# Values of mixer D: blocks of consecutive tokens and a store and load through DRAM in place of strided columns

## The chip, the cores and the metric

The kernel runs on one core of a Trainium2 chip. The metric is the device time of one execution in microseconds (us). A core has a matrix engine (TensorE, PE in the profile, its loads of the stationary operand shown apart as PEld), a vector engine (DVE), a scalar engine (ACT), a general engine (POOL) and a queue engine (SP) that issues DMA transfers. Each engine works through its own instructions in order and waits on semaphores for the others.

## The reference

Two layers over 512 tokens of width 1024. A layer computes one wide projection, four mixers A, B, C and D, a gated sum of their projections, and an MLP. Only mixer D and its values matter here:

```python
proj = hn @ w_in[l]                      # dv: 3 groups x 4 heads x 64 = 768 columns of it
def mixer_d(q, k, v, cs):                # v: [b, s, 3 groups, 4 heads, 64]
    for gi, (window, dil) in enumerate(((128, 1), (512, 4), (2048, 16))):
        # tokens of one residue modulo dil attend to each other, in a band
        o, lse = banded_attention(to_residue(q), to_residue(k), to_residue(v), window // (2 * dil), 64)
    # groups combined by their softmax denominators
```

The first group uses the tokens in their natural order, the other two by residues.

## The kernel before

All products are done in parts: each operand is split into a high and a low part, and one product becomes three (high by high, high by low, low by high; lines 177 to 179 in `mm3`). The 1024 channels are 8 blocks of 128, so a full product is 24 matrix instructions. `xh` and `xl` hold the normed input, split, as [128 channels, 8 blocks, 512 tokens].

The weights come as a stream of chunks of 128 x 1024 (512 KB): a load on SP's queue into one of three raw buffers (`wload`, line 102), a cast by ACT that makes the high part (`whi`, line 118), and a subtraction by DVE that makes the low part (`wlo`, line 127). `take` hands a chunk out and issues the casts and loads that come next. There are three buffers of split chunks, so the cast of a later chunk waits until the chunk three places ahead of it is used up.

The layer has phases. In phase 1 the projections are made. Then each attention (A, C, D) is interleaved by `merge` with a "fill" of matrix products that do not depend on it: gates and branch projections of a mixer that is done. The interleave is counted: `MG` gives for each phase the attention's steps, the fill's steps and how many fill steps come ahead. In the phase of mixer C the fill is `values_d` followed by `fill(l, 0, yA)`, and the entry is (41, 73, 2).

`values_d` (line 669) makes the values of mixer D, three groups (two chunks of weights each, `take2`). In it the tokens are the stationary operand (the columns of `xh` that are loaded into the array) and the 256 value columns of the group are the moving one. A token chunk is one product of 24 instructions, in two fill steps of 12. The keys of each group lie in an own order of tokens, and the value rows are made directly in that order:

- first group: five chunks, of 64, 128, 128, 128 and 64 consecutive tokens (`off`, line 671);
- second and third group: four chunks each, every fourth token from residue c on (`slice(c, None, 4)`, line 679).

ACT takes each result out of PSUM into the tile `VD` with a factor per token (lines 685 and 686). PSUM gives these products two buffers in turn (`ps("mm")`). The factors lie in `roff` in the same orders as the tokens; `roff` is filled in phase 1 by three small loads from DRAM (lines 465 to 467). Attention D (`attn_d`) reads `VD` as stationary operand in the phase after that of mixer C (lines 992 and 998).

`fill` takes its gate tiles `gt` from a pool of five buffers (line 731). Loads of mixer C's queries (line 773) go through SP's queue between the weight loads.

Of the kernel before, what the change touches and what calls it, by code (L numbers as in the profile page):

```python
# [11 lines left out]
F32 = mybir.dt.float32  # L12
# [16 lines left out]
V_GMIX, V_GMLP, V_GB, V_CW, V_CB, V_LGB, V_LAM, V_G, V_SINK = 0, 8, 16, 48, 64, 68, 84, 92, 96  # L29
NV = 104  # L30
# [4 lines left out]
# attention of A and C: the stages of a step and how many steps each lags behind the first  # L35
# [4 lines left out]
# steps of an attention phase, steps of its fill, steps of the fill ahead of the first one  # L40
MG = ((35, 48, 3), (41, 73, 2), (18, 47, 12))
# waits in the end of mixer D, in steps of the fill beside it, and the steps of that fill
E1, E2, E3, FN = (1, 5, 2, 15)
# products that warm the tensor engine up; parts in which the first two chunks come
WU, P0, P1 = (16, 2, 2)
# the order of the projections; pieces of mixer B after each; projections that its gates follow
# [29 lines left out]
class Body:  # L76
# [29 lines left out]
    def parts(self, i):  # L106
        """the first chunk is worked on in parts, for an early start"""
        n = (P0, P1, 1)[min(i, 2)]
        return [slice(p * (1024 // n), (p + 1) * (1024 // n)) for p in range(n)]
# [20 lines left out]
    def ahead(self, i):  # L130
        """the high parts of the next groups, and the loads beyond them"""
        i -= self.held
        n = len(self.order)
        while self.n_split < min(i + self.HLB, n):
            self.whi()
        while self.n_load < min(self.n_lo + self.RAWB, n):
            self.wload()
# [5 lines left out]
    def take2(self, *key):  # L143
        """two chunks that stay for several groups"""
        return [self.take(*key, u, wide=u) for u in range(2)]
# [38 lines left out]
    def several(self, keys, mv, cuts):  # L184
        """the groups of some chunks, side by side: each part of the depth for all of them"""
        sts = [self.wst(self.take(*key, wide=u)) for u, key in enumerate(keys)]
        pss = [self.wide() for _ in keys]
        mm = self.nc.tensor.matmul
        for k0, k1 in zip((0,) + cuts, cuts + (KD,)):
            for st, ps in zip(sts, pss):  # L190
                for k in range(k0, k1):
                    (sh, sl), (mh, ml) = st(k), mv(k)
                    mm(ps, sh, mh, start=(k == 0), stop=False)
                    mm(ps, sh, ml, start=False, stop=False)
                    mm(ps, sl, mh, start=False, stop=(k == KD - 1))
        self.ahead(self.n_take)
        self.lows()
        return pss
# [22 lines left out]
    def rsqrt(self, v, n, tag):  # L221
        """v: [128, n] in SBUF, positive"""
        nv = self.nc.vector
        y, t = self.smt(n, tag + "y"), self.smt(n, tag + "t")
        yi = y.bitcast(I32)
        nv.tensor_scalar(out=yi, in0=v.bitcast(I32), scalar1=1, scalar2=None, op0=ALU.logical_shift_right)
        nv.tensor_scalar(out=yi, in0=yi, scalar1=-1.0, scalar2=float(0x5F3759DF), op0=ALU.mult, op1=ALU.add)
        for _ in range(3):
            nv.scalar_tensor_tensor(out=t, in0=y, scalar=-0.5, in1=y, op0=ALU.mult, op1=ALU.mult)
            nv.tensor_tensor(out=t, in0=t, in1=v, op=ALU.mult)  # L230
            nv.scalar_tensor_tensor(out=y, in0=t, scalar=1.5, in1=y, op0=ALU.add, op1=ALU.mult)
        return y

    def xg_tile(self, xt, c, gcol):
        """xt [128, 512] f32: tile c of the residual; writes xg"""
        nc = self.nc
        nc.scalar.activation(out=self.xh[:, c], in_=xt, func=AF.Copy, scale=gcol)
        nc.vector.scalar_tensor_tensor(
            out=self.xl[:, c], in0=xt, scalar=gcol, in1=self.xh[:, c].bitcast(F32), op0=ALU.mult, op1=ALU.subtract
        )  # L240
# [10 lines left out]
    def norm_cols(self):  # L251
        """1/rms of each token, as columns [128, 4]"""
        nc = self.nc
        ps = self.misc()
        for c in range(4):
            nc.tensor.matmul(ps[:, c:c + 1], self.acc[:, c * 128:(c + 1) * 128], self.ones[:, 0:1])
        v = self.smt(4, "nv")
        nc.vector.tensor_scalar(out=v, in0=ps[:, 0:4], scalar1=1.0 / DM, scalar2=EPS, op0=ALU.mult, op1=ALU.add)
        return self.rsqrt(v, 4, "n")
# [38 lines left out]
    def derive(self):  # L298
# [7 lines left out]
        # softplus(-lam) = max(-lam, 0) + log1p(exp(-|lam|)), log1p(u) = 2 atanh(u / (u + 2))  # L306
# [23 lines left out]
    # ================= projections of the mixers, and mixer B =================  # L330
    def rope(self, X1, X2, T, dst, split, perm=False):
        """X1, X2 in PSUM; T: the factors (of x1, of x2 in the first half; of x2, of x1 in the second)"""
# [64 lines left out]
    def phase1(self, l):  # L397
# [13 lines left out]
        self.kD = self.drp.tile([3, 4, 64, S], F32, tag="kD", name="kD")  # L411
        ckp, skp = self.table(4, "b0"), self.table(5, "b1")
# [12 lines left out]
        def head_scale(key, nh, sel, n=128):  # L425
            """1/rms of each head and token, but for the token's own factor: [128, 4 * nh]"""
# [21 lines left out]
        # the tokens' 1/rms, as columns, as a row, and over all partitions  # L448
# [12 lines left out]
        # tokens in other orders: by 64 from 64 on for the first group of D, by residues for the others  # L461
        rd = self.drp.tile([S], F32, tag="rd", name="rd")
        self.roff = self.mixp.tile([128, 16], F32, tag="roff", name="roff")
        nc.sync.dma_start(out=rd.rearrange("(o n) -> o n", o=1), in_=row)
        nc.sync.dma_start(out=self.roff[:, 8:12], in_=rd.rearrange("(p r) -> p r", r=4))
        nc.sync.dma_start(out=self.roff[:, 1:4], in_=rd[64:448].rearrange("(c p) -> p c", p=128))
        nc.sync.dma_start(out=self.roff[0:64, 0:5:4], in_=rd.rearrange("(c p) -> p c", p=64)[:, 0:8:7])
# [41 lines left out]
        # queries of C, queries and keys of D; gates of mixer B between them  # L509
# [16 lines left out]
        nv.tensor_scalar(out=self.rs8p, in0=self.roff[:, 8:12], scalar1=0.125, scalar2=None, op0=ALU.mult)  # L526

    def values_ac(self):
        """values of A and C: token-major, [hi | lo]"""
# [68 lines left out]
    def gates_b(self, f):  # L598
        """gates of a tile of mixer B; what follows goes to the queue"""
# [33 lines left out]
        def s2(f, d):  # L633
            q, a, u = bs[f, d]
            # 1 - a^2 = tanh(-log a) (1 + a^2)
            nv.scalar_tensor_tensor(out=q, in0=Tg[f, d, 0], scalar=1.0, in1=q, op0=ALU.add, op1=ALU.mult)
            nv.scalar_tensor_tensor(out=u, in0=u, scalar=1.0, in1=self.xcs[f], op0=ALU.add, op1=ALU.mult)
# [31 lines left out]
    def values_d(self):  # L669
        ns = self.nc.scalar  # L670
        off = ((0, 64), (64, 192), (192, 320), (320, 448), (448, 512))
        last = []
        for g in range(3):
            hls = self.take2("VD", g)
            for c in range(5 if g == 0 else 4):
                if g == 0:
                    sl, n, col = slice(*off[c]), off[c][1] - off[c][0], c
                else:
                    sl, n, col = slice(c, None, 4), 128, 8 + c
                ps = self.ps("mm")  # L680
                yield from self.paced(last, self.mm3(
                    ps[0:n, 0:256],
                    lambda k: (self.xh[:, k, sl], self.xl[:, k, sl]),
                    lambda k: tuple(t[:, (k % 4) * 256:(k % 4 + 1) * 256] for t in hls[k // 4]), KD, 4))
                last.append(lambda ps=ps, n=n, i=(0, 5, 9)[g] + c, col=col: ns.activation(
                    out=self.VD[0:n, i], in_=ps[0:n, 0:256], func=AF.Copy, scale=self.roff[0:n, col:col + 1]))
                yield
        while last:
            last.pop()()

# [8 lines left out]
    # ================= gates and projections of the branches =================  # L699
# [44 lines left out]
    # ================= attention =================  # L744
    def pipeline(self, steps, order):
        """steps: dicts of stages; order: (stage, its distance in steps from the first)"""
# [7 lines left out]
    def attn_gqa(self, l, which, y):  # L754
        """8 heads, 2 key heads. A: all keys; C: a band, with sinks"""
# [274 lines left out]
    def attn_d_end(self, y):  # L1030
        """the groups' weights: exp(m_g - M) / sum_g l_g exp(m_g - M)"""
# [57 lines left out]
    def merge(self, a, b, na, nb, first=0):  # L1089
        """a's first step, a few of b, then na steps of a spread over nb of b; then the rest"""  # L1090
# [19 lines left out]
    # ================= the layer =================  # L1110
    def layer(self, l):
# [99 lines left out]
        def last(h):  # L1211
            """the last two tiles and the final norm, by halves of the tokens"""
# [255 lines left out]
```

## Time and profile before

| | us |
|---|---|
| time, median of 3 runs | 2096.09 |
| lowest, highest | 2095.13, 2098.7 |
| span of the profiled execution, first to last instruction | 2091.4 |
| median less that span | 4.7 |
| PE busy | 2071.0 (99%) |
| PEld busy | 1711.7 (82%) |
| DVE busy | 1273.3 (61%) |
| ACT busy | 977.9 (47%) |
| DMA queue q1, share of 16 engines | 31.6% |

The profile is of one execution, and its span is what the rows below add up to; the time of a run also holds some us around it. Matrix instructions overlap: one is shown as 0.28 us long and the next starts 0.12 us after it. So the pace of TensorE is read from the starts of instructions that follow each other, not from their lengths. A wait in the profile names the waiting instruction, then what released it, the sum in us, how often, and the longest.

### The profile page before, as it was taken

Reading aid. Unit: us, or ns where it says so; the run is one execution under the profiler, and the core shown is the slowest. Engines: PE = TensorE matmul, PEld = TensorE weight load, DVE = VectorE, ACT = ScalarE, POOL = GpSimd, SP = SyncE. Lnnn points to the kernel's source line nnn. Section 1 sums busy time; section 2 is a strip of 40 time slices with the busy share of each in tenths; the row PEclk is TensorE's granted clock in tenths of the full one; section 3 lists DMA queues with packets and bytes.
Section 4 is the critical chain, followed back from the end, with each engine's and each line's share of the span. In section 5 each row is a group of like instructions: output and inputs, shape, how many; then the busy total and the mean of one; then the engine's idle time right before and its main releaser. Section 6 shows DMA issues by size and latency. Waiting matters only on the chain.

```text
span 2091.4 us, 25718 instructions
## 1 busy us (share of the span) xinstructions
PE 2071.0 (99%) x9800; PEld 1711.7 (82%) x9800; DVE 1273.3 (61%) x2274; ACT 977.9 (47%) x1703; POOL 0.2 (0%) x4
## 2 busy tenths in 40 slices
PE   9999999999999999999999999999999999999997
PEld 7888889987778888888878888898877788888886
DVE  6889774575466544444658887736644665444445
ACT  4366885663534332322323667757545343322322
POOL 0000000000000000000000000000000000000000
PEclk9999999999999999999999999999999999999999
DMA  5445313122234222222325552312321432223221
GB/s 190 156 142 159 113 54 100 59 97 95 72 100 144 95 97 94 97 93 99 133 95 171 159 163 67 101 66 66 121 81 53 135 117 93 99 93 99 93 100 61
DMA packets 83407, 220.74 MB, mean 106 GB/s; under 512 B 15674, under 2 KB 17850, under 8 KB 83284
## 3 DMA queue, kind: packets, MB, share of 16 engines
q1 hardware_dynamic: 80404, 214.91, 31.6%
q10 hardware_dynamic: 2880, 4.20, 0.6%
q8 instruction: 77, 1.26, 0.3%
q14 instruction: 46, 0.38, 0.1%
HBM read 197.94 MB, written 21.12 MB: 105 GB/s over the span
## 4 chain that ended last, share of the span: by engine, by line
PE 96%; DVE 2%; ACT 1%; issue 1%; DMA 0%; SPq 0%; DVEq 0%; ACTq 0%
PE ps_mm L177 15%; PE ps_mm L179 14%; PE ps_mm L178 14%; PE ps_t L177 6%; PE ps_t L179 6%; PE ps_t L178 6%; PE ps_s L177 6%; PE ps_s L179 6%; PE ps_s L178 6%; PE ps_o L846 2%; PE ps_t L825 2%; PE ps_s L786 1%; PE ps_s L787 1%; PE ps_o L992 1%; PE ps_t L966 1%; PE ps_s L917 1%
## 5 line engine op out<-in xcount | busy, mean ns | idle before, releaser
L118 ACT CAST whi<-raw 128x1024 fp32r<-128x1024 f32 (+1 forms) x318 | 329.9, 1042 | 353.6 <-PE ps_mm L178 122.0
L127 DVE TENSOR_TENSOR wlo<-raw,whi 128x1024 fp32r<-128x1024 f32 (+1 forms) x318 | 385.0, 1214 | 106.0 <-ACT whi L118 103.3
L177 PE MATMUL ps_mm<-xh,whi 128*128 128x512 f32 x720 | 288.2, 400 | 0.0
L179 PE MATMUL ps_mm<-xh,wlo 128*128 128x512 f32 x720 | 282.0, 392 | 0.0
L178 PE MATMUL ps_mm<-xl,whi 128*128 128x512 f32 x720 | 281.8, 391 | 0.0
L177 PEld LDWEIGHTS ps_mm<-xh,whi 128*128 128x128 f32 x720 | 135.5, 188 | 32.4 <-issue 4.1
L179 PEld LDWEIGHTS ps_mm<-xh,wlo 128*128 128x128 f32 x720 | 135.6, 188 | 29.3
L178 PEld LDWEIGHTS ps_mm<-xl,whi 128*128 128x128 f32 x720 | 135.8, 189 | 26.9
L177 PE MATMUL ps_t<-xh,whi 128*128 128x512 f32 x368 | 143.7, 390 | 0.0
L178 PE MATMUL ps_t<-xl,whi 128*128 128x512 f32 x368 | 143.2, 389 | 0.0
L179 PE MATMUL ps_t<-xh,wlo 128*128 128x512 f32 x368 | 143.2, 389 | 0.0
L177 PE MATMUL ps_s<-xh,whi 128*128 128x512 f32 x352 | 138.6, 394 | 0.0
L179 PE MATMUL ps_s<-xh,wlo 128*128 128x512 f32 x352 | 137.1, 389 | 0.0
L178 PE MATMUL ps_s<-xl,whi 128*128 128x512 f32 x352 | 137.0, 389 | 0.0
L835 DVE TENSOR_TENSOR PT<-ps_t,PT 128x512 fp32r<-128x512 f32 (+2 forms) x128 | 75.2, 588 | 72.2 <-ACT PT L832 56.6
L832 ACT CAST PT<-ps_t 128x512 fp32r<-128x512 f32 (+2 forms) x128 | 63.8, 501 | 57.5 <-PE ps_o L846 56.1
L819 ACT ACTIVATE P<-P,al 128x512 f32<-128x512 f32 (+2 forms) x128 | 82.7, 646 | 12.6 <-DVE al L818 11.6
L709 DVE TENSOR_TENSOR gt<-ps_mm,rb 128x512 f32<-128x512 f32 x54 | 37.2, 688 | 80.7 <-PE ps_mm L179 80.5
L177 PEld LDWEIGHTS ps_t<-xh,whi 128*128 128x128 f32 x368 | 69.1, 188 | 17.4 <-issue 3.0
L179 PEld LDWEIGHTS ps_t<-xh,wlo 128*128 128x128 f32 x368 | 69.1, 188 | 14.4
L178 PEld LDWEIGHTS ps_t<-xl,whi 128*128 128x128 f32 x368 | 69.1, 188 | 14.3
L177 PE MATMUL ps_mm<-whi,xh 128*128 128x256 f32 (+1 forms) x224 | 79.6, 355 | 0.0
(423 smaller groups left out, 4330.7 us busy)
## 6 DMA issues: line engine op xcount, KB each, us to landing
raw<-in_w_dram SPq DMA_DIRECT2D x314, 512.0 KB, 3.5
qsA<-stk SPq DMA_DIRECT2D x32, 128.0 KB, 2.3
qsC<-stk SPq DMA_DIRECT2D x32, 128.0 KB, 2.3
K<-ks SPq DMA_DIRECT2D x16, 256.0 KB, 5.6
Q<-qsA SPq DMA_DIRECT2D x16, 256.0 KB, 4.0
Q<-qsC SPq DMA_DIRECT2D x16, 256.0 KB, 2.7
qD<-stkf SPq DMA_DIRECT2D x24, 128.0 KB, 2.2
kD<-stkf SPq DMA_DIRECT2D x24, 128.0 KB, 2.2
```

Of the source, the lines that this page charges most:

```text
L118: self.nc.scalar.copy(hi[:, s], self.raws[i][:, s])
L127: self.nc.vector.tensor_tensor(out=lo[:, s], in0=raw[:, s], in1=hi[:, s].bitcast(F32), op=ALU.subtract)
L177: mm(ps, sh, mh, start=(k == 0), stop=False)
L178: mm(ps, sh, ml, start=False, stop=False)
L179: mm(ps, sl, mh, start=False, stop=(k == n - 1))
L709: nv.tensor_tensor(out=g, in0=ps, in1=self.rb, op=ALU.mult)
L786: nc.tensor.matmul(ps[:, 0:n], qq, Kt[j][:, 0, b0 * 128:b1 * 128], start=True, stop=False)
L819: ns.activation(out=P[:, 0:n], in_=P[:, 0:n], func=AF.Copy, scale=ls)
L825: nc.tensor.transpose(pt[:, b * 128:(b + 1) * 128], P[:, b * 128:(b + 1) * 128], self.ident)
L832: ns.copy(st["dst"][0], st["src"])
L835: nv.tensor_tensor(out=st["dst"][1], in0=st["src"], in1=st["dst"][0].bitcast(F32), op=ALU.subtract)
L846: nc.tensor.matmul(o, a, b, start=(n_ == 0), stop=(n_ == len(mm) - 1))
```

## The change

Every token chunk of `values_d` is now one of four blocks of 128 consecutive tokens, for all three groups. The result leaves PSUM by ACT into a staging tile `vst` (one of the five `gt` buffers, 256 of its columns) with the factor of the natural token order, `rcol`. SP stores it to a DRAM tensor `vD`. After the fourth chunk of a group SP loads the group back into `VD` in the order of its keys: two loads for the first group, one for each other group. `roff` shrinks to the four columns that attention D needs, and two of its three loads go. The fill's step count in `MG` goes from 73 to 71.

```diff
-MG = ((35, 48, 3), (41, 73, 2), (18, 47, 12))
+MG = ((35, 48, 3), (41, 71, 2), (18, 47, 12))
...
+        self.vD = self.drp.tile([3, S, 256], F32, tag="vD", name="vD")
...
-        self.roff = self.mixp.tile([128, 16], F32, tag="roff", name="roff")
+        self.roff = self.mixp.tile([128, 4], F32, tag="roff", name="roff")
         nc.sync.dma_start(out=rd.rearrange("(o n) -> o n", o=1), in_=row)
-        nc.sync.dma_start(out=self.roff[:, 8:12], in_=rd.rearrange("(p r) -> p r", r=4))
-        nc.sync.dma_start(out=self.roff[:, 1:4], in_=rd[64:448].rearrange("(c p) -> p c", p=128))
-        nc.sync.dma_start(out=self.roff[0:64, 0:5:4], in_=rd.rearrange("(c p) -> p c", p=64)[:, 0:8:7])
+        nc.sync.dma_start(out=self.roff, in_=rd.rearrange("(p r) -> p r", r=4))
...
-        nv.tensor_scalar(out=self.rs8p, in0=self.roff[:, 8:12], scalar1=0.125, scalar2=None, op0=ALU.mult)
+        nv.tensor_scalar(out=self.rs8p, in0=self.roff, scalar1=0.125, scalar2=None, op0=ALU.mult)
...
     def values_d(self):
-        ns = self.nc.scalar
-        off = ((0, 64), (64, 192), (192, 320), (320, 448), (448, 512))
+        nc = self.nc
         last = []
         for g in range(3):
             hls = self.take2("VD", g)
-            for c in range(5 if g == 0 else 4):
-                if g == 0:
-                    sl, n, col = slice(*off[c]), off[c][1] - off[c][0], c
-                else:
-                    sl, n, col = slice(c, None, 4), 128, 8 + c
+            for c in range(4):
                 ps = self.ps("mm")
                 yield from self.paced(last, self.mm3(
-                    ps[0:n, 0:256],
-                    lambda k: (self.xh[:, k, sl], self.xl[:, k, sl]),
+                    ps[:, 0:256],
+                    lambda k: (self.xh[:, k, c * 128:(c + 1) * 128], self.xl[:, k, c * 128:(c + 1) * 128]),
                     lambda k: tuple(t[:, (k % 4) * 256:(k % 4 + 1) * 256] for t in hls[k // 4]), KD, 4))
-                last.append(lambda ps=ps, n=n, i=(0, 5, 9)[g] + c, col=col: ns.activation(
-                    out=self.VD[0:n, i], in_=ps[0:n, 0:256], func=AF.Copy, scale=self.roff[0:n, col:col + 1]))
+                last.append(lambda ps=ps, g=g, c=c: self.value_d(ps, g, c))
                 yield
...
+    def value_d(self, ps, g, c):
+        nc = self.nc
+        t = self.gtp.tile([128, S], F32, tag="gt", name="vst", bufs=5)
+        nc.scalar.activation(out=t[:, 0:256], in_=ps[:, 0:256], func=AF.Copy, scale=self.rcol[:, c:c + 1])
+        nc.sync.dma_start(out=self.vD[g][c * 128:(c + 1) * 128], in_=t[:, 0:256])
+        if c < 3:
+            return
+        if g == 0:
+            nc.sync.dma_start(out=self.VD[:, 1:4], in_=self.vD[g][64:448].rearrange("(c p) n -> p c n", p=128))
+            nc.sync.dma_start(
+                out=self.VD[0:64, 0:5:4], in_=self.vD[g].rearrange("(c p) n -> p c n", p=64)[:, 0:8:7]
+            )
+        else:
+            o = (5, 9)[g - 1]
+            nc.sync.dma_start(out=self.VD[:, o:o + 4], in_=self.vD[g].rearrange("(p r) n -> p r n", r=4))
```

The rest of the diff takes comments and docstrings out.

## Rows read from the trace of the kernel before

**Rows 1.** Page, part 4: the chain that ended last, share by engine.
```profile
PE 96%; DVE 2%; ACT 1%; issue 1%; DMA 0%; SPq 0%; DVEq 0%; ACTq 0%
```

**Rows 2.** Waits of PE, whole span: us in total, times, longest.
```profile
PE ps_s L786 <- DMA Q<-qsA: 5.6, 2, 3.4
...
PE ps_s L1256 <- ACT dg L1252: 1.7, 1, 1.7
```

**Rows 3.** Stretches: length; PE, PEld, DVE, ACT, POOL busy (instructions); PEclk; DMA; GB/s.
```profile
223.00:318.00 95.00, 95.00 (x473) 77.88 (x472) 70.69 (x148) 75.72 (x141) 0.00 (x0) 1.00 0.24 78
318.00:332.00 14.00, 14.00 (x113) 13.72 (x112) 6.90 (x23) 8.38 (x20) 0.00 (x0) 1.00 0.42 103
332.00:390.00 58.00, 58.00 (x292) 57.53 (x291) 21.97 (x71) 29.35 (x72) 0.00 (x0) 1.00 0.17 58
390.00:505.00 115.00, 115.00 (x556) 94.89 (x554) 77.88 (x192) 66.94 (x148) 0.00 (x0) 1.00 0.30 100
```

**Rows 4.** Timeline of PE, first group's values: start, length, instruction.
```profile
319.16 0.28 PE L177 MATMUL ps_mm<-whi,xh 128*64 128x256 f32 x1
...
321.78 0.28 PE L179 MATMUL ps_mm<-whi,xl 128*64 128x256 f32 x1
...
327.13 0.28 PE L177 MATMUL ps_mm<-whi,xh 128*128 128x256 f32 x1
...
329.88 0.28 PE L179 MATMUL ps_mm<-whi,xl 128*128 128x256 f32 x1
```

**Rows 5.** Timeline of PE, second group's values (every fourth token).
```profile
353.02 0.40 PE L178 MATMUL ps_mm<-wlo,xh 128*128 128x256 f32 x1
...
358.15 0.40 PE L179 MATMUL ps_mm<-whi,xl 128*128 128x256 f32 x1
```

**Rows 6.** Weight loads, ns min/median/max: consecutive tokens (values of A, C), every fourth.
```profile
L179 PEld LDWEIGHTS ps_mm<-whi,xl x8: 192/192/192, 197.3 to 199.9; 128*128 128x128 f32 x8
...
L179 PEld LDWEIGHTS ps_mm<-whi,xl x40: 329/329/329, 339.8 to 371.6; 128*128 128x128 f32 x40
```

**Rows 7.** Groups by shape, 318 to 390: count, busy us and mean ns, idle before.
```profile
L178 PE MATMUL ps_mm<-wlo,xh 128*128 128x256 f32 x88 | 32.1, 365 | 0.0
L685 ACT ACTIVATE VD<-ps_mm,roff 128x256 f32<-128x256 f32 x11 | 5.2, 471 | 16.4 <-PE ps_mm L179 16.4
L178 PE MATMUL ps_mm<-wlo,xh 128*64 128x256 f32 x16 | 4.5, 279 | 0.0
```

**Rows 8.** DMA issues: count, KB each, median us from issue to landing.
```profile
raw<-in_w_dram SPq DMA_DIRECT2D x314, 512.0 KB, 3.5
qD<-stkf SPq DMA_DIRECT2D x24, 128.0 KB, 2.2
Kd<-kD SPq DMA_DIRECT2D x6, 512.0 KB, 5.8
```

**Rows 9.** Timelines of ACT, DVE and PE where the first group ends.
```profile
334.41 2.16 ACT L118 CAST whi<-raw 128x1024 fp32r<-128x1024 f32 x2
335.48 2.36 DVE L127 TENSOR_TENSOR wlo<-raw,whi 128x1024 fp32r<-128x1024 f32 x2 [1.42 <-ACT whi L118]
339.03 0.40 PE L178 MATMUL ps_mm<-wlo,xh 128*128 128x256 f32 x1
```

**Rows 10.** Timelines of SP and ACT: raw chunks issued, and cast.
```profile
360.92 3.80 SPq L102 DMA_DIRECT2D raw<-in_w_dram  x2
388.31 1.99 ACT L118 CAST whi<-raw 128x1024 fp32r<-128x1024 f32 x2
```

**Rows 11.** Waits of all engines, whole span: ACT for raw chunks.
```profile
ACT whi L118 <- DMA raw<-in_w_dram: 13.4, 7, 4.7
```

**Rows 12.** Timeline of SP: the two small loads of phase 1.
```profile
28.74 0.42 SPq L466 DMA_DIRECT2D roff<-rd  x1
29.20 0.68 SPq L467 DMA_DIRECT2D roff<-rd  x1
```

**Rows 13.** The tile VD: its readers, ns min/median/max, first and last start.
```profile
L992 PEld LDWEIGHTS ps_o<-ptd,VD x128: 129/136/137, 507.9 to 1584.1; 128*64 128x64 f32 x96, 64*64 64x64 f32 x32
```

## The prediction

> **What bounds the kernel now.** I read the chain of work that ended last first: 96% of it is TensorE, and no DMA and no queue has a share worth a percent [rows 1]. Then the waits of PE over the whole span: there are five kinds, from 5.6 us down to 1.7 us, 13.5 us together, all at the start, the end and at the seams of phases; none is in the phase where the values of mixer D are made [rows 2]. Then the stretches around that phase. From 318 to 390 us, where the values of D are made, PE is busy throughout, ACT for 8.38 + 29.35 = 37.7 of 72 us, DVE for 28.9; the granted clock is 1.00, which is 2.4 GHz, before, in and after it [rows 3]. So the time of this stretch is the sum of PE's instructions, and what the change is worth is how much faster PE can issue them, as long as the others keep up.
>
> The pace is read from starts. In the first group, whose tokens are consecutive, a chunk of 128 tokens starts its first instruction at 327.13 and its 24th at 329.88: 2.75 / 23 = 0.1196 us each. A chunk of 64 tokens goes from 319.16 to 321.78: 0.1139 us each, hardly less, since the 256 moving columns are the same [rows 4]. In the second group, with every fourth token, the starts from 353.02 to 358.15 hold 22 steps in 5.13 us: 0.2332 us each [rows 5]. Shape and moving data are those of the 128-token chunk before it; only the step between the stationary columns differs, and with it the weight load, 329 ns against 192 ns for consecutive tokens [rows 6]. PEld is busy for 57.5 of 58 us between 332 and 390, and only for 94.9 of 115 us in the stretch behind [rows 3]. There the weight load is the limit, and it is so because of the step.
>
> **The change part by part.** In one layer the phase has 88 x 3 = 264 instructions of 128 tokens and 16 x 3 = 48 of 64 [rows 7]. Of the 264, three chunks of 24, that is 72, are the first group's; 192 are strided.
>
> Strided to consecutive: 192 x (0.2332 - 0.1196) = 21.8 us less a layer.
>
> Five chunks to four in the first group: 48 x 0.1139 = 5.47 us go, 24 x 0.1196 = 2.87 us come, 2.6 us less. Together 24.4 us a layer and 48.8 us in two layers, all of it on the path, since PE never waits here. Against the profiled execution: span 2091.4 - 48.8 = 2042.6 us. The runs shown have 2095.13 to 2098.7 us, so 3.7 to 7.3 us lie around the span; I keep the median's 4.7 and get 2047.3 us.
>
> Here a rule of the Trainium skill speaks against the change. The rows above show 329 ns against 192 ns for loads of the same 128 columns [rows 6]. "TensorE: Matmul & The Clock Gate", section "LDWEIGHTS (loading the stationary operand)", times a weight load by its number of columns alone, and "SBUF — State Buffer", section "Door 1: The DMA port swizzle", says that a reader may step up to four fp32 values for free. By these the strided groups would gain nothing. The trace disagrees, and I go by it.
>
> ACT's evictions: 13 of about 0.47 us become 12 of the same shape into another tile [rows 7]; each still follows half a chunk behind its product. Nothing gained or lost on PE. They share five gate buffers with the fill, and a buffer must have been stored before the fifth chunk after it: about 20 us, against 2.2 us for a store of 128 KB [rows 8]. If that cover were gone, ACT would wait, and behind it the exponentials of mixer C.
>
> Stores and loads: 12 stores of 128 KB and four loads (384, 128 and twice 512 KB) a layer, all on SP. A store waits there for its eviction, a load for the landing of the group's fourth store, at about 2.2 us each by the nearest row; a load lands after up to 5.8 us [rows 8]. Queued behind them on SP are the queries of mixer C and the raw chunks. The two raw chunks that are issued at 360.9 are cast at 388.3, 27 us ahead [rows 10]. With a group shortened to about 16 us they are still some 16 us ahead, against 2.2 us of waiting and 3.5 us to land. `take2` issues a pair's raw loads before the old group's last store, so they do not stand behind its load. The first reader of `VD` comes at 507.9 us [rows 13], and the last load will be issued near 366 us. Cost nought. The other bound: a late chunk holds ACT for up to 4.7 us now [rows 11], and none of it shows as a wait of PE [rows 2]; if one came in each layer and passed on whole, 9.4 us.
>
> What gets tight is the cast at the seam of two groups. There are three split chunks and a group needs two, so the second chunk of the next group can be cast only when the old group's first is done, half a chunk ahead of the seam. At the first seam the two casts start at 334.41, the low part of the first is done near 335.48 + 2.36 / 2 = 336.7, and PE needs it at 339.03: 2.3 us to spare with the strided pace [rows 9]. At the new pace half a chunk is 12 x (0.2332 - 0.1196) = 1.4 us shorter, which leaves about 0.9 us there. At the second seam the old half chunk gets shorter too, but casts there start just when the buffer is free. There are four seams in all. Cost between nought and 1.6 us each: the cast and the low part are 1.08 + 1.18 us [rows 9], and one attention step ahead of them in ACT's queue is worth 37.7 us / 14 steps = 2.7 us [rows 3]; from release to need there are two halves, 24 x 0.12 = 2.9 us, and some 0.4 us of scores between them, so 2.7 + 2.3 - 3.3 = 1.7 us at worst, less the 0.1 us or so by which the high part is needed first. I take 0.25 us each, near the margin that the rows show, so 1.0 us in all: 2048.3 us. The bounds are nought and 6.4 us. A late raw chunk would delay the same casts, so the two upper bounds do not add up, and 9.4 us is the greater.
>
> The two small loads that go from phase 1 took SP 0.42 and 0.68 us [rows 12]. PE waits for nothing there, so I count nothing; if the weight loads behind them were on the path, 2.2 us in two layers would be gained. The fill of the phase shrinks from 26 + 48 to 24 + 48 steps, and its count from 73 to 71, so the attention is spread as before (1.73 fill steps for each of its own, 1.78 before): no change.
>
> **The rivals.** First, the scalar engine becomes the bound of the shortened stretch. PSUM has two buffers for these products, so the eviction of a chunk must be done half a chunk and an attention step after it was queued, about 1.43 + 0.7 us. ACT's work for an attention step is 2.7 us, and were it always ahead of the eviction, with 0.47 us on top, each chunk would lose about 0.6 us after what the next step gives back: 24 chunks, 14 us, 2062 us. For it: 37.7 us of ACT in 72 - 24.4 = 47.6 us is 79%. Against it: from 223 to 318 us ACT is at 75.7 of 95 us, 80%, with longer attention steps, and PE is busy throughout [rows 3].
>
> Second, the step is not what costs: the slow pace belongs to something that stays (the place in the interleave, the chunk of weights). Then only the fifth chunk of the first group is saved, 2 x 2.6 us: 2090.9 us. Both pages named above would have it so. Against it: the pace is slow from the first strided chunk on and back to normal after it, and the moving operands are of the same kind.
>
> Third, slower: SP's queue, worked through in order, starves the weight stream. At the end of a group SP waits for a store to land (2.2 us), and if the load behind it (5.8 us) and a raw chunk (3.5 us) followed one after the other with PE standing, a group would cost 11.5 us, six of them 69 us: 2047.3 + 69 = 2116 us. It decides from the point where a raw chunk is issued less than 11.5 us before its cast, and it is slower than before if more than 8 of the 11.5 us reach PE. Against it: the 27 us ahead of now, and DMA engines busy 17% from 332 to 390 [rows 3, 10].
>
> **How the numbers follow.** The forecast, PE's sum with small losses at the seams, gets 0.86; ACT as bound 0.09; the step not the cause 0.02; starvation 0.03. The predicted time is the forecast's, 2048.3. The range: from 2047.3 less the 2.2 us of the small loads and some tenths of scatter, 2044, to 2047.3 + 9.4, 2057. It holds nearly all of the forecast's 0.86; the rivals lie beyond. About 0.2%, 4 us, is what a measurement of this kernel can tell from no change. Faster by more: forecast, ACT's case and half of the 0.02 (5.2 us is just beyond 0.2%), 0.96; within: 0.01; slower: 0.03.
>
> **What would show it.** Right: all 288 instructions of the values in a layer start 0.12 us apart, weight loads of 192 ns; the stretch that held them is 47 to 49 us instead of 72; PE's waits have no new entry beyond a few us in all. ACT shows about 79% in it. The loads into `VD` land more than 100 us ahead of their reader. Wrong: a wait of PE for the low part or for a cast at the seams beyond 1.6 us (the seam cost), a wait of PE for the eviction's PSUM buffer (first rival), starts still 0.23 us apart (second), or waits of ACT for raw chunks between 318 and 390 us, of which there should be none (third).

## The result and the profile after

The changed kernel takes 2046.53 us (median of 4 runs, 2045.1 to 2046.72) against 2096.04 us in the runs beside it: ratio 0.9762, 95% interval 0.9748 to 0.9776. The forecast was 2048.3 us, with 2044 to 2057 as range. The profiled execution has a span of 2043.3 us, 48.1 us less than that of [rows 1 to 3]; the forecast's own sum was 2042.6 plus 1.0 at the seams.

The weight loads while the values of D are made, first layer (the tile `ps_mm` on PEld, 320.8 to 366.2 us: count, ns min/median/max, first and last start); [rows 6] had 329 ns:

```profile
L178 PEld LDWEIGHTS ps_mm<-wlo,xh x96: 186/192/192, 320.8 to 365.9; 128*128 128x128 f32 x96
L179 PEld LDWEIGHTS ps_mm<-whi,xl x96: 187/192/192, 321.0 to 366.1; 128*128 128x128 f32 x96
```

The pace in the second group, read as in [rows 5] from the second to the last of the 24 starts of a chunk:

```profile
338.84 0.28 PE L178 MATMUL ps_mm<-wlo,xh 128*128 128x256 f32 x1
...
341.47 0.28 PE L179 MATMUL ps_mm<-whi,xl 128*128 128x256 f32 x1
```

These are 22 steps in 2.63 us, 0.1195 us each, where the second group had 0.2332. A chunk of the third group, from 354.96 to 357.59, has the same.

The stretches from the first instruction of the values of D to the first one of the gates behind them, in both layers after and, for comparison, the first layer before (columns as in [rows 3]):

```profile
320.85:366.30 45.45, 44.55 (x361) 43.74 (x360) 25.12 (x84) 32.28 (x81) 0.00 (x0) 1.00 0.51 152
1330.90:1376.36 45.46, 44.56 (x361) 43.75 (x360) 25.13 (x84) 32.27 (x81) 0.00 (x0) 1.00 0.49 152
```
```profile
319.16:388.21 69.05, 69.05 (x389) 68.84 (x388) 27.82 (x90) 35.95 (x89) 0.00 (x0) 1.00 0.21 66
```

69.05 us became 45.45. The granted clock is 1.00 in all three. PE is no longer busy throughout: 0.9 us is idle. The DMA engines went from 21% to 51%: the stretch is shorter, and each layer now stores 1.5 MB and loads 1 MB in it (another 0.5 MB is loaded just behind it).

All waits of PE in the span after (us in total, times, longest):

```profile
PE ps_s L796 <- DMA Q<-qsA: 4.4, 2, 2.2
PE ps_misc L1313 <- ACT ones L285: 2.3, 1, 2.3
PE ps_misc L1068 <- DVE w L1064: 2.0, 2, 1.0
PE ps_misc L1252 <- ACT sq L1245: 1.9, 1, 1.9
PE ps_s L1266 <- ACT dg L1262: 1.7, 1, 1.7
PE ps_mm L178 <- DVE wlo L127: 1.3, 2, 0.7
PE ps_t L835 <- DVE PT L845: 0.5, 2, 0.2
```

The first five are those of [rows 2]; the first of these fell from 5.6 to 4.4 us. The last two are new, once in each layer. The wait for `wlo` is at the first seam, which the prediction called tight. Here are PE, then ACT, then DVE around it (start, length, instruction):

```profile
331.70 0.28 PE L179 MATMUL ps_mm<-whi,xl 128*128 128x256 f32 x1
...
335.58 0.28 PE L179 MATMUL ps_mm<-whi,xl 128*128 128x256 f32 x1
335.70 0.28 PE L177 MATMUL ps_mm<-whi,xh 128*128 128x256 f32 x1
336.63 0.38 PE L178 MATMUL ps_mm<-wlo,xh 128*128 128x256 f32 x1 [0.65 <-DVE wlo L127]
```
```profile
332.92 0.62 ACT L829 ACTIVATE P<-P,al 128x384 f32<-128x384 f32 x1
333.50 0.60 ACT L820 ACTIVATE P<-P,an,rs 128x256 f32<-128x256 f32 x1
334.01 0.18 ACT L820 ACTIVATION_READ_ACCUMULATOR P<-P,an,rs 128x1 f32 x1
334.10 0.28 ACT L822 ACTIVATE ae<-an,ve 128x1 f32<-128x1 f32 x1
334.28 1.98 ACT L118 CAST whi<-raw 128x1024 fp32r<-128x1024 f32 x2
```
```profile
335.35 2.36 DVE L127 TENSOR_TENSOR wlo<-raw,whi 128x1024 fp32r<-128x1024 f32 x2 [1.55 <-ACT whi L118]
```

The instruction at 335.70 uses the high part, the next one the low part of the same chunk, and that is half of what DVE begins at 335.35. The cast at 334.28 is not late because its buffer is: the old group's first chunk has its last use in the instruction at 331.70, some 2.3 us before. ACT works without a gap through the normalisation and the exponentials of an attention step of mixer C first.

At the second seam PE waits for no cast and no low part, but the other new wait stands just behind it. The low parts hold DVE up, so it reads the transposes of attention C out of PSUM late (`PT<-ps_t`), and PE waits for that buffer (PE, then DVE):

```profile
354.59 0.41 PE L835 MATMUL ps_t<-cs,P 128*128 128x128 f32 x2 [0.25 <-DVE PT L845]
```
```profile
350.71 2.36 DVE L127 TENSOR_TENSOR wlo<-raw,whi 128x1024 fp32r<-128x1024 f32 x2 [1.79 <-ACT whi L118]
...
353.90 0.55 DVE L845 TENSOR_TENSOR PT<-ps_t,PT 128x384 fp32r<-128x384 f32 x1
```

The way through DRAM, on SP's queue (start, length, issue):

```profile
338.16 0.38 SPq L689 DMA_DIRECT2D vD<-vst  x1
342.69 0.38 SPq L693 DMA_DIRECT2D VD<-vD  x1
...
364.26 3.06 SPq L689 DMA_DIRECT2D vD<-vst  x2
368.75 0.32 SPq L699 DMA_DIRECT2D VD<-vD  x1
371.47 0.32 SPq L783 DMA_DIRECT2D Q<-qsC  x1
373.98 22.68 SPq L102 DMA_DIRECT2D raw<-in_w_dram  x5
```

After the last store of a group SP stands until it has landed, and only then issues the load: for 4.2 and 4.6 us after the first two groups, and for 1.4 us after the third, whose last store is issued near 367.0. The sizes and landing times between 318 and 368 us (count, KB each, median us):

```profile
raw<-in_w_dram SPq DMA_DIRECT2D x6, 512.0 KB, 5.1
vD<-vst SPq DMA_DIRECT2D x12, 128.0 KB, 4.5
```

The stores differ among themselves: two that are issued between 327 and 332.1 us, where the DMA engines are 11% busy, land after 1.7 us in the median, and three between 353.4 and 360 us, where they are 65% busy, after 5.0 us.

### The profile page after: what moved, and what is told of

Read it like the earlier page. It is cut to its first block, busy times and chain, and to the rows that moved or that the text cites. A ratio compares the mean times of both kernels' runs of the same rounds, so it can differ in the third digit from the quotient of the medians.

```text
span 2043.3 us, 25698 instructions
## 1 busy us (share of the span) xinstructions
PE 2023.1 (99%) x9752; PEld 1664.0 (81%) x9752; DVE 1270.7 (62%) x2274; ACT 975.0 (48%) x1701; POOL 0.2 (0%) x4
## 4 chain that ended last, share of the span: by engine, by line
PE 97%; DVE 1%; DMA 1%; ACT 1%; issue 0%; SPq 0%; DVEq 0%; ACTq 0%
PE ps_mm L177 14%; PE ps_mm L179 14%; PE ps_mm L178 14%; PE ps_t L177 7%; PE ps_t L179 7%; PE ps_t L178 7%; PE ps_s L177 6%; PE ps_s L179 6%; PE ps_s L178 6%; PE ps_o L856 2%; PE ps_t L835 2%; PE ps_s L796 1%; PE ps_s L797 1%; PE ps_o L1002 1%; PE ps_t L976 1%; PE ps_s L927 1%
## 5 line engine op out<-in xcount | busy, mean ns | idle before, releaser
L178 PEld LDWEIGHTS ps_t<-xl,whi 128*128 128x128 f32 x368 | 69.1, 188 | 14.2
L177 PEld LDWEIGHTS ps_s<-xh,whi 128*128 128x128 f32 x352 | 66.1, 188 | 14.9 <-issue 1.4
```

## The experiments

The whole time of a run also holds what differs outside of the change, so two readings are given for each kernel: its time, and one stretch of its profile, from the first value product of attention A (`ps_o`) to the first score product of attention D. It holds all of the values of D and all of the attention that is spread around them. Before it is 257.80 us in both layers, and in a second profile of the same program 257.79 and 257.77. For a look at how the first layer's stretch is made up, before and after (columns as in [rows 3]):

```profile
231.12:488.92 257.80, 257.80 (x1318) 225.64 (x1316) 161.81 (x388) 166.21 (x348) 0.00 (x0) 1.00 0.26 85
```
```profile
232.85:467.33 234.48, 233.58 (x1294) 200.89 (x1292) 160.69 (x388) 165.32 (x347) 0.00 (x0) 1.00 0.34 108
```

| kernel | time, us | ratio to before (95%) | stretch, layer 1 | layer 2 |
|---|---|---|---|---|
| before, again | 2096.17 | 1.000 (0.9991 to 1.0009) | 257.79 | 257.77 |
| changed | 2046.53 | 0.9762 (0.9748 to 0.9776) | 234.48 | 234.43 |
| first group only | 2085.87 | 0.995 (0.9936 to 0.9965) | 255.12 | 255.06 |
| first group only, again | 2086.91 | 0.996 (0.9946 to 0.9973) | 255.06 | 255.06 |
| first group only, direct | 2087.96 | 0.9961 (0.9949 to 0.9974) | 255.06 | 255.06 |
| no way through DRAM | 2044.26 | 0.9754 (0.9738 to 0.977) | 234.48 | 234.46 |
| loads three times | 2055.7 | 0.981 (0.9795 to 0.9824) | 236.44 | 241.98 |
| evictions twice | 2047.34 | 0.9766 (0.975 to 0.9782) | 234.81 | 234.83 |
| count 73, small loads back | 2045.59 | 0.9762 (0.9747 to 0.9776) | 234.77 | 234.77 |
| steps 2 and 3 | 2063.16 (one run) | | 241.44 | 241.41 |
| steps 8 and 6 | 2098.28 (one run) | | 258.03 | 258.03 |

**The first group alone.**

```diff
             for c in range(4):
+                sl = slice(c * 128, (c + 1) * 128) if g == 0 else slice(c, None, 4)
...
     def value_d(self, ps, g, c):
+        if g > 0:
+            nc.scalar.activation(out=self.VD[:, (5, 9)[g - 1] + c], in_=ps[:, 0:256], func=AF.Copy, scale=self.roff[:, c:c + 1])
+            return
```

> Only the first group of values takes four blocks of 128 consecutive tokens and the way through DRAM; the second and third group keep every fourth token and go straight into VD. Theory (the step between the stationary columns is what costs): the strided 192 instructions of a layer keep their 0.233 us, so only the fifth chunk's 2.6 us a layer go: 5.2 us, ratio 0.9975, about 2091 us. Rival (the gain comes from the interleave, the step count 71 or the eviction into a staging tile, not from the step): a good part of the 49 us shows here too, under 2080 us.

The stretch shrank by 2.68 and 2.74 us, as the sum of 2.6 us has it. The time fell by 10.9 us, twice what was expected. Since the stretch said one thing and the time another, three more sets were taken.

> The kernel before, unchanged, as one of the kernels that are compared, to see how far two sets of runs of one program lie apart and to have a second profile of it. Theory and rival alike: ratio 1.000, within 0.1%.

> The first group alone in four blocks through DRAM once more, since its first set came out 10.9 us faster than before where 5.2 were expected, while the stretch from the first to the last value product of a layer's attentions A and C was 2.65 us shorter in each layer, as expected. Theory (the excess is scatter outside of that stretch): the ratio comes out nearer to 0.9975, between 0.996 and 0.999. Rival (the first group's change brings something more, outside of that stretch): again 0.995 or less.

The third writes the first group straight into `VD`:

```diff
-        t = self.gtp.tile([128, S], F32, tag="gt", name="vst", bufs=5)
...
+        nc.scalar.activation(out=self.VD[:, c], in_=ps[:, 0:256], func=AF.Copy, scale=self.rcol[:, c:c + 1])
...
+        nv.memset(self.VD[0:64, 4], 0.0)
```

> As the first group alone in four blocks, but written straight into VD, with no store and load: the reordering of the first group for its keys is left out and its fifth block is zero. Theory (the stores and loads cost and bring nothing): the time of the kernel with the round trip for the first group within 2 us. Rival (the excess of 5 us in that kernel comes with the stores and loads): 5 us slower than it, 2091 us.

The program of before, compared with itself, gives 1.000 within 0.0009. The first group alone gives 0.996 again, with and without the way through DRAM (0.9958 and 0.9961). So the second set falls between what theory and rival expected of it, just outside of both. The third comes within the 2 us that its theory allowed: the stores and loads bring nothing. The fall of the time is 10.9, 8.9 and 7.8 us in the three sets, 2.4 to 5.5 us more than the 5.4 us of the two stretches. A part of this excess can be placed: in the second layer, from the first value product of A and C to the first score of attention A, both profiles of before need 15.09 us and every kernel with four blocks in the first group 13.9 to 14.2 us, with a wait of PE at its end of 3.4 us before, for the queries of A, and of 2.2 to 2.5 us after, for the queries or for DVE. Why that wait is shorter was not found. It bears on the changed kernel as well: some 1.2 us of its 48.1 us lie there and not in the values of D.

The rest is not placed, but the two profiles of before show where such differences can come from. Their spans are 2091.4 and 2095.1 us, and their stretches are equal. In the second profile the granted clock is at its lower level, 1.2 GHz, for a while near 42 and near 1247 us (the mean granted clock of a stretch is the third number from the end); in the first one it is not. The second profile, then the first:

```profile
40.00:46.00 6.00, 6.00 (x28) 5.11 (x28) 5.52 (x22) 0.94 (x1) 0.00 (x0) 0.72 0.27 87
1246.00:1251.00 5.00, 4.95 (x15) 3.94 (x16) 4.97 (x10) 4.97 (x8) 0.00 (x0) 0.66 1.01 284
```
```profile
40.00:46.00 6.00, 6.00 (x31) 5.07 (x31) 5.52 (x22) 0.00 (x0) 0.00 (x0) 1.00 0.31 90
```

By an estimate from these rows that is 6 x 0.28 + 5 x 0.34 = 3.4 of the 3.7 us. PE was at work before the first fall; before the second it had waited 3.4 us for the queries of A, as it did in the first profile without a fall. Over the 11 runs of that set the shortest three have a mean granted clock of 0.997 and the longest one 0.995. How much of the excess is of this kind can't be told, since each other kernel has one profile.

**No way through DRAM.**

```diff
-        t = self.gtp.tile([128, S], F32, tag="gt", name="vst", bufs=5)
-        nc.scalar.activation(out=t[:, 0:256], in_=ps[:, 0:256], func=AF.Copy, scale=self.rcol[:, c:c + 1])
-        nc.sync.dma_start(out=self.vD[g][c * 128:(c + 1) * 128], in_=t[:, 0:256])
...
+        nc.scalar.activation(out=self.VD[:, (0, 5, 9)[g] + c], in_=ps[:, 0:256], func=AF.Copy, scale=self.rcol[:, c:c + 1])
...
+        nv.memset(self.VD[0:64, 4], 0.0)
```

> All three groups in blocks of consecutive tokens, but ACT writes them straight into VD in that order, with no store and no load; the reordering for the keys is left out, so mixer D gets its values in another order, and the fifth block of the first group is zero. Theory (the round trip is hidden whole): the time of the changed kernel, 2046.5 us within 2, weight loads of 192 ns. Rival (the waits of SP for landings cost something on the path): faster than the changed kernel by over 4 us.

The stretches are equal to 0.03 us. The median time is 2.3 us lower, a little beyond the 2 of the theory and short of the 4 of the rival, and the times overlap (2043.54 to 2046.98 against 2045.1 to 2046.72). By the stretches, twelve stores and four loads a layer cost nothing on the path.

**Loads three times.**

```diff
-        if g == 0:
+        for _ in range(3):
+            self.load_d(g)
+
+    def load_d(self, g):
+        nc = self.nc
+        if g == 0:
```

> The changed kernel with every load from vD into VD issued three times, each waiting for the landing of the one before, so that SP's queue stands some 8 us longer at the end of each group. Theory (the raw chunks are issued some 16 us ahead, and nothing else on SP is pressing): at most 3 us slower than the changed kernel, under 2050 us. Rival (SP's queue is close to starving the weight stream): most of six times 8 us shows, 2080 to 2095 us, with waits of ACT for raw chunks.

It came out 9.2 us slower than the changed kernel, beyond the 3 us that the theory allowed, and far from the rival's 48. The stretches are longer by 1.96 and 7.55 us, 9.5 together, and the waits of PE name one new entry:

```profile
PE ps_o L861 <- ACT PT L847: 6.0, 2, 4.7
```

That wait is 1.4 us in the first layer and 4.7 us in the second. SP's queue and ACT's cast behind the last group, second layer:

```profile
1386.91 7.46 SPq L704 DMA_DIRECT2D VD<-vD  x3
1394.42 0.43 SPq L788 DMA_DIRECT2D Q<-qsC  x1
1394.95 10.03 SPq L102 DMA_DIRECT2D raw<-in_w_dram  x4
```
```profile
1401.07 1.04 ACT L118 CAST whi<-raw 128x1024 fp32r<-128x1024 f32 x1 [6.51 <-DMA raw<-in_w_dram]
```

This is the mechanism of the third rival: the raw chunk stands behind the loads into `VD`, its cast waits 6.51 us for it, ACT's later work (the copies for attention C) with it, and PE for that. The wait is not the whole cost: while PE stands, the granted clock falls, and when PE goes on it is at 0.50, 1.2 GHz, for some 5.4 us. In the 5 us from 1403 it starts 16 instructions where the changed kernel starts 25 in 5 us of the same phase:

```profile
1403.00:1408.00 5.00, 4.95 (x16) 4.39 (x17) 4.01 (x10) 3.22 (x9) 0.00 (x0) 0.50 0.36 105
```
```profile
1398.00:1403.00 5.00, 5.00 (x25) 4.15 (x25) 3.57 (x13) 4.32 (x11) 0.00 (x0) 1.00 0.18 75
```

By an estimate from these rows half of 5.4 us is lost, 2.7 us; with the 4.7 us of waiting that makes 7.4 of the second layer's 7.55. In the changed kernel the load of the last group is issued at 368.75 and the next raw chunk at 373.98, 5.2 us later, when its buffer comes free; its cast is at 382.49, 8.5 us after the issue. So the chunk that matters is the first one behind the last group, and the queue has about 5 us of slack there before that issue moves at all.

**Evictions twice.**

```diff
         nc.scalar.activation(out=t[:, 0:256], in_=ps[:, 0:256], func=AF.Copy, scale=self.rcol[:, c:c + 1])
+        nc.scalar.activation(out=t[:, 256:512], in_=ps[:, 0:256], func=AF.Copy, scale=self.rcol[:, c:c + 1])
```

> The changed kernel with every result of the values of D taken out of PSUM twice by ACT, the second time into the unused half of the staging tile: 24 more activations of about 0.47 us. Theory (ACT has room in the stretch, 33 of 48 us busy): at most 2 us slower than the changed kernel, 2046.5 to 2048.5 us, the seam's wait a little longer. Rival (ACT is close to the bound of the shortened stretch): most of 24 x 0.47 = 11 us shows, about 2058 us.

The stretches grow by 0.33 and 0.40 us for 5.6 us of added work of ACT in each. The first seam's wait grows from 0.7 to 0.9 us. ACT is not near the bound; the first rival falls.

**The count and the small loads back.**

```diff
-MG = ((35, 48, 3), (41, 71, 2), (18, 47, 12))
+MG = ((35, 48, 3), (41, 73, 2), (18, 47, 12))
...
+        nc.sync.dma_start(out=self.roff[:, 1:4], in_=rd[64:448].rearrange("(c p) -> p c", p=128))
+        nc.sync.dma_start(out=self.roff[0:64, 0:5:4], in_=rd.rearrange("(c p) -> p c", p=64)[:, 0:8:7])
```

> The changed kernel with the fill's count back at 73 and the two small loads of token factors back in phase 1 (nothing reads them). Theory: both are worth nothing, 2046.5 us within 2. Rival (a part of the gain sits in the spread of the attention's steps or in the small loads ahead of the weight loads): slower by over 4 us.

The time is the same within the theory's 2 us; the stretch is 0.3 us longer in each layer. The two edits together are worth nothing that the times can tell.

**Other steps between the columns.** In the kernel before:

```diff
-                    sl, n, col = slice(c, None, 4), 128, 8 + c
+                    sl, n, col = (slice(c % 2 + c // 2 * 256, c % 2 + c // 2 * 256 + 255, 2) if g == 1 else slice(c, c + 382, 3)), 128, 8 + c
```

> The kernel before, but the second group takes every second token and the third every third one instead of every fourth; the values then stand beside other keys than the reference's. Theory (a weight load reads lines of 16 bytes, and a step of four values finds a new one for each column): step 2 runs at 0.12 us an instruction with a weight load near 192 ns; step 3 lies between 0.12 and 0.233 us. Rival (any step costs the same): both at 0.233 us and 329 ns. Second rival (the cost grows evenly with the step): weight loads of about 238 and 283 ns, paces of about 0.14 and 0.19 us.

Weight loads of the second group (step 2) and of the third (step 3):

```profile
L178 PEld LDWEIGHTS ps_mm<-wlo,xh x25: 194/196/198, 340.9 to 353.0; 128*128 128x128 f32 x25
```
```profile
L179 PEld LDWEIGHTS ps_mm<-whi,xl x28: 261/265/265, 355.9 to 373.6; 128*128 128x128 f32 x28
```

The pace, read as in [rows 5] from the second start to the last: a whole chunk at step 2, then half a chunk at step 3.

```profile
349.18 0.28 PE L178 MATMUL ps_mm<-wlo,xh 128*128 128x256 f32 x1
...
351.82 0.28 PE L179 MATMUL ps_mm<-whi,xl 128*128 128x256 f32 x1
```
```profile
361.54 0.34 PE L178 MATMUL ps_mm<-wlo,xh 128*128 128x256 f32 x1
...
363.29 0.34 PE L179 MATMUL ps_mm<-whi,xl 128*128 128x256 f32 x1
```

Step 2: 2.64 / 22 = 0.120 us, as for consecutive tokens. Step 3: 1.75 / 10 = 0.175 us, three quarters of the 0.2332 us of step 4. Both rivals fall in their numbers. But steps 1 to 4 can't tell whether a load pays for lines of 16 bytes (four values; step 3 touches a new line with three columns out of four) or for the distance. So steps beyond a line were tried, across the blocks of `xh` taken as one row:

```diff
...
+        step = (8, 6)[g - 1]
+        o = min(k, 5) * 512 + c
+        return t.rearrange("p k t -> p (k t)")[:, o:o + 127 * step + 1:step]
```

> The kernel before, but the stationary columns of the second group are eight values apart and those of the third six, taken across the blocks of the input as if it were one row; their values are thus sums over mixed channels and tokens, of no meaning, and only the pace is looked at. With the paces found for steps 1, 2, 3 and 4 (0.120, 0.120, 0.174 and 0.233 us) two readings agree so far. Reading one (a weight load pays for each line of 16 bytes it touches, at 0.233 / 128 = 1.82 ns): step 6 and step 8 touch 128 lines as step 4 does, so 0.233 us and 329 ns in both, and the time of before, 2096 us within 3. Reading two (the load pays for the distance it walks, 0.058 us a value of step): 0.35 us at step 6 and 0.47 us at step 8, 96 x (0.117 + 0.233) = 34 us a layer more, about 2163 us.

Weight loads at step 8, then at step 6:

```profile
L178 PEld LDWEIGHTS ps_mm<-wlo,xh x16: 337/338/342, 339.7 to 351.2; 128*128 128x128 f32 x16
```
```profile
L178 PEld LDWEIGHTS ps_mm<-wlo,xh x18: 322/323/341, 365.0 to 377.7; 128*128 128x128 f32 x18
```

338 and 323 ns, next to 329 at step 4; the starts are 0.241 and 0.229 us apart, next to 0.2332; and the one run took 2098.28 us, against 2097.3 beside it. Reading one holds to 4%, and reading two, with 0.47 and 0.35 us, falls: the cost stops growing where each column has a line of its own.

## Why the prediction was right, point by point

**The bound.** PE's issue was the limit and stayed it. All but 0.9 us of the 234.48 us stretch is PE at work.

**Strided to consecutive, 21.8 us a layer.** The weight loads of all groups went to 192 ns, and the starts in the second and third group to 0.1195 us apart. With the fifth chunk's 2.6 us the sum was 24.4 us a layer. The stretch shrank by 23.32 and 23.37 us, and with the new 0.9 us of waiting added back, by 24.2 to 24.3. The fifth chunk alone gave 2.7 us by the stretch. The second rival, by which the step costs nothing, falls. With it fall the two rules of the Trainium skill that stood beside it: "TensorE: Matmul & The Clock Gate", section "LDWEIGHTS (loading the stationary operand)", counts columns alone, but loads of 128 columns took 192, 196, 265, 329, 323 and 338 ns at steps 1, 2, 3, 4, 6 and 8; "SBUF — State Buffer", section "Door 1: The DMA port swizzle", lets four fp32 go for free, but only a step of two does. The same passage says that two hits to a line are needed for full speed, and that part the runs bear out.

**The seams, 1.0 us in all.** PE waits 0.65 us at the first seam of each layer and 0.25 us just behind the second, 1.8 us in all, well inside the bounds of nought and 6.4. The step behind the chosen value was off. I left about 0.9 us to spare at the first seam, from the cast's place in the kernel before; at the new pace PE came there 0.65 us too early, because ACT still had some 2.3 us of an attention step to do between the release of the buffer and the cast. That was the upper bound's case, not the chosen one. The wait behind the second seam, for DVE's work on attention C, was not in the working. That 1.0 us came as near as it did is thus in part luck.

**Stores and loads, nothing.** The result holds (no way through DRAM: the same stretch; the last load of the first layer lands near 372 us, and the first reader of `VD` comes at 486.3), the grounds only in part. A store landed after 4.5 us in the median and not 2.2: after 1.7 us where the DMA engines were 11% busy, after 5.0 us where they were 65% busy. And the 16 us ahead were true of a chunk that I followed, not of the first chunk behind the last group, with 5.2 us of slack on SP. The trace of before already had that chunk. With the 318 loads and casts counted through in order, the chunk issued at 396.14 is cast at 405.52, 9.4 us ahead, less than the 11.5 us at which the prediction let that rival begin:

```profile
396.14 1.47 SPq L102 DMA_DIRECT2D raw<-in_w_dram  x2
```
```profile
405.52 1.03 ACT L118 CAST whi<-raw 128x1024 fp32r<-128x1024 f32 x1
```

By the same count only the first of the two chunks issued at 360.92 belongs to the pair of casts at 388.31; the second is cast at 396.02. The load threefold showed that rival's mechanism at work once the slack is used up.

**ACT at 79%.** It is 32.28 of 45.45 us, 71%: 14 steps of attention fall into the shorter stretch where 15 did before. The conclusion stood.

**From the span to the time.** I put 4.7 us around the span, the median less the profiled span. In every run whose span is on record the time is only 1.7 to 1.9 us longer than its own span. The other 2.9 us are there because the profiled execution of before was a quick one: 2091.4 us, where the eleven runs of the second set have spans of 2091.3 to 2097.2. Adding 4.7 us did the forecast no harm, since it only led back to the median. From median to median the time fell by 49.5 us where 48.8 - 1.0 = 47.8 were forecast. The two stretches gave 46.7 of it, 1.1 less than that; the other 2.8 us lie outside of them, where the prediction had no term and the cause stays open beyond the 1.2 us named above. So the mechanism and its size were right, and most of the 1.8 us by which the forecast is too high comes from outside of what it looked at.

## What to carry to other kernels

Where weight loads fill PE's time, look at the step between the stationary columns: compare the starts of two products of the same shape, one with consecutive columns and one without, in the same trace. A reorder of a small result through DRAM can be free where its reader is far away, but what it costs is decided on the queue that issues it: find the first transfer that stands behind its waits and how long before its use that is issued. Take the time around the span from the run that was profiled, not from the median of others. And a wait of the matrix engine can cost more than its length: look at the granted clock behind it.

## What the runs showed of the hardware

- A weight load of 128 fp32r columns took 192, 196, 265 and 329 ns at steps of 1, 2, 3 and 4 values, and 323 and 338 ns at 6 and 8. The paces of 0.175 and 0.2332 us at steps 3 and 4 stand as 96 to 128, the number of 16-byte lines that the columns touch: 1.82 ns a line. At step 2 that would be 0.117 us by this estimate; the pace there was 0.120, the same as at step 1.
- A store of 128 KB landed after 1.7 us where the DMA engines were 11% busy and after 5.0 us where they were 65% busy.
- In the kernel with the loads threefold the granted clock fell to 0.50 in a wait of PE of 4.7 us and stayed there for some 5.4 us after it. After waits of 3.4 us it fell in one profile of before and not in the other.
